# A second pair of up-projection blocks by seven half-size products, and another engine for the opening's ones

## The chip, the cores and the metric

The kernel runs on one core of a Trainium2 chip. The engines are TensorE (PE in the profile; its weight loads are the row PEld), VectorE (DVE), ScalarE (ACT), GpSimd (POOL) and SyncE (SP), which issues most DMAs. Each engine works through its own queue in order and waits on semaphores for the others. The metric is the device time of one execution in microseconds; the median of three runs counts.

## The reference

A two-layer encoder on 512 tokens of width 1024, all in float32. Each layer normalizes, projects, runs three token mixers, gates and merges them, and then applies a convolutional feed-forward block. The change is in the feed-forward block:

```
def conv_ffn(h, w_up, conv_w, conv_b, w_down):
    u = h @ w_up
    C = u.shape[-1]
    u = lax.conv_general_dilated(u, conv_w[:, None, :].astype(u.dtype), window_strides=(1,),
                                 padding=((CONV_W // 2, CONV_W // 2),),
                                 dimension_numbers=('NWC', 'WIO', 'NWC'),
                                 feature_group_count=C) + conv_b
    a, g = jnp.split(u, 2, axis=-1)
    return (jax.nn.gelu(g) * a) @ w_down

def reference(x, ...):
    for l in range(DEPTH):
        h = rmsnorm(x, norm1_g[l])
        x = x + gated_parallel_mixer(h, w_in[l], ...)
        h = rmsnorm(x, norm2_g[l])
        x = x + conv_ffn(h, w_up[l], conv_w[l], conv_b[l], w_down[l])
    return rmsnorm(x, final_g)
```

The up projection is 1024 x 5632: 22 blocks of 128 columns for the half `a` and 22 for the gate half `g`.

## The kernel before

**Products.** Activations stand transposed, 128 channels by 512 tokens. Every float32 operand is split into a high part (fp32r) that ScalarE casts and a low part, the rest, that VectorE subtracts (`split`, lines 208 and 209). A product is three matmuls per 128 channels: high by high, high by low, low by high (`mm3`). For weights the two parts are the tiles `whi` and `wlo`, with three buffers each (`WB`); the raw weights come by SP's queue into `raw`, with three buffers too (`RAWB`). `fetch` issues loads and splits a few weights ahead of their use. The low part of the weights is read by the third matmul of each 128 channels.

**An up block** f of one half (`do_up`) is 8 x 3 matmuls of 512 columns into one PSUM bank, which `conv` reads on ScalarE (line 1113) and twice on VectorE (lines 1115, 1116). A gate block ends in a gelu (line 1120) and a product with its partner (`prod`), and `operands` makes the transformed halves for the down projection (tiles `tt` and `ft`, lines 1141 to 1155).

**A unit** (`do_us`) takes two neighbouring blocks of one half at once. It splits the 2 x 2 block matrix of weights (256 columns by pairs of 128 channels) and the activations (two halves of 256 tokens) as in Strassen's scheme with seven products in place of eight. Each product is 4 x 3 matmuls of 256 columns; the order of the weights is V11, S1, V12, S2, S4, V22, S3. The sums S1 and S3 of raw weights are made by adding DMAs from GpSimd's queue (lines 173, 174), S2 and S4 by VectorE (lines 189, 192). `load_sum` loads V22, V21 (as S1) and V11 into the tiles `own`, `s1`, `own`, and V21 again and V12 into two of the three `raw` buffers; V21's buffer becomes S3 and is held to the last product. The transformed activations are four `hs` tile sets, made once a layer from `hx` (`mix`, `sums4`, lines 1044 to 1048) while blocks 13 and 14 are issued. The tuple `UPS` names the units: before, only blocks 18 and 19 of the gate half.

**Order.** TensorE's and SP's queues follow the program (`schedule`); `ups` alternates the halves. A unit stands where its second block stood. On VectorE and ScalarE a list scheduler places the instructions of blocks 6 and up when the kernel is built; splits of weights have a high priority. In the order before, the blocks of f 16 to 19 are issued as 16a, 16g, 17a, 17g, 18a, 19a, unit 18/19g.

**Banks.** There are eight PSUM banks. In the feed-forward part the group `d` rotates through 0, 1, 2, 3, 4, 5, 7, 6; a dense block takes one, a unit or a sum of the down projection four. Layer 1 opens (`do_mla_open`) with banks 0 to 3 for the first four products, whatever the rotation left. The last sum of layer 0 ends with VectorE's read at line 1185.

**Opening.** Seven idle matmuls (line 432) read a tile of ones, `early`, while the first loads are under way.

Of the kernel before, what the change touches and what calls it, by code (L numbers as in the profile page):

```python
# [24 lines left out]
EPS = 1e-6  # L25
# [14 lines left out]
NP, AHEAD, EVAC = (6, 5, 4), (7, 4), 400  # L40
F2 = 2 * NP[0]
FIX = 6
UPS = ((9, 1),)
ORDERS = (("V11", "S1", "V12", "S2", "S4", "V22", "S3"), ("V11", "V12", "S1", "S2", "S4", "V22", "S3"))
B11, B21, B22, T1, T3, T2, T4 = range(7)
ROWS = (slice(0, 64), slice(64, 128))
# [19 lines left out]
class Trunk:  # L66
# [5 lines left out]
    def __init__(self, ctx, tc, d):  # L72
        self.tc, self.nc, self.d, self.ctx = tc, tc.nc, d, ctx
        nc = self.nc
        self.small = ctx.enter_context(tc.tile_pool(name="small", bufs=1))
        self.const = ctx.enter_context(tc.tile_pool(name="const", bufs=1))
        self.wp = ctx.enter_context(tc.tile_pool(name="wp", bufs=1))
        self.psum = ctx.enter_context(tc.tile_pool(name="psum", bufs=1, space=bass.MemoryType.PSUM))
        self.groups, self.turn = {}, {}
        c = self.const  # L80
        x0 = c.tile([P, S + NPC], F32, name="x0")
        self.x = [x0[:, :S]] + [c.tile([P, S], F32, name=f"x{k}") for k in range(1, KD)]
        self.par = [x0[:, S:], self.small.tile([P, NPC], F32, name="par1")]
        self.early = c.tile([P, P], F32, tag="acc", name="early")
        nc.vector.memset(self.early, 1.0)
        self.idf = c.tile([P, P], F32, name="idf")
        make_identity(nc, self.idf)
        self.mean = c.tile([P, P], F32R, name="mean")
        cst = self.small.tile([P, 7], F32, name="cst")
        self.neghalf, self.ones = cst[:, 0:4], cst[:, 4:5]  # L90
        nc.vector.memset(self.neghalf, -0.5)
        nc.vector.memset(self.ones, 1.0)
        self.eps = cst[:, 6:7]
        nc.vector.memset(self.eps, EPS)
        self.warm = cst[:, 5:6]
        nc.scalar.activation(self.warm, self.ones, AF.Exp)
        self.specs, self.raws, self.parts, self.used = [], {}, [], 0
        self.plans = [self.schedule(l) for l in range(L)]
        for s, W in self.plans:
            self.specs += [w for item in s for w in W.get(item, ())]  # L100
        nc.sync.dma_start(x0[:, :S + PC_CW], d["x0"])
        self.fetch(1, 0)
        for k in range(1, 5):
            nc.sync.dma_start(self.x[k], d["xT"][k * P:(k + 1) * P, :])
            self.fetch(min(k + 1, 3), 0)
        self.gmask = self.small.tile([P, 3 * P], BF16, name="gmask")
# [223 lines left out]
    def schedule(self, l):  # L330
# [30 lines left out]
        for f in ups[8:]:  # L361
            W["up", f] = [(d["w_up"][l], 0, KD, f * P, P)]
        for i, p in UPS:
            unit = {"w": d["w_up"][l], "m": p * NF + 2 * i, "part": 1, "np": 4, "r0": 0, "order": ORDERS[0]}
# [33 lines left out]
        seq[n - 8:n - 8] = [("sum", 0, m) for m in range(0, KD, 2)]  # L398
        for i, p in UPS:
            old = [("up", p * NF + 2 * i + e) for e in range(2)]  # L400
# [97 lines left out]


    def do_mla_open(self):  # L500
        self.banks(g=[0, 1, 2, 3], d=[4, 5, 0, 1, 2, 3], r=[6, 7])
        self.mxs, self.mx = self.open("mx")
        self.mps, self.mp = self.open("ml")
        self.mp2 = self.mps.enter_context(self.tc.tile_pool(name=f"mm{self.l}", bufs=1, reuse_waits="tile"))
        self.rc, self.rsn = (self.mp.tile([P, S], F32, tag=t, name="rope", bufs=2) for t in ("knh", "knl"))
        if self.l:
            self.rope_table()
        self.hb = self.small.tile([P, 24], F32, tag="hb", name="hb")
        self.nc.vector.tensor_scalar(self.hb, self.pr[:, PC_BG:PC_BG + 24], 0.5, None, ALU.mult)
        self.merged, self.z = [None] * KD, {}  # L510
        self.qn, self.kn, self.pts, self.pp, self.y = {}, {}, {}, {}, {}
# [27 lines left out]
    def do_lat4(self):  # L539
        if self.l == 0:  # L540
            rest = self.par[0][:, PC_CW:]
            for t, src in ((rest, self.d["par"][0][:, PC_CW:]), (self.par[1], self.d["par"][1])):
                self.nc.gpsimd.tensor_copy(t[:, 0:4], self.rt)
                self.nc.gpsimd.dma_start(t, src)
            self.nc.gpsimd.tensor_scalar(self.mean, self.idf, 0.0, 1.0 / D, ALU.mult, ALU.add)
        self.latent(4, self.dense(self.spec(), self.h))

# [609 lines left out]
    def do_sum(self, part, m):  # L1157
# [33 lines left out]
        elif m == KD - 2:  # L1191
# [3 lines left out]
            for _ in self.operands(F2):  # L1195
                pass
            if UPS:
                self.whole()
# [219 lines left out]
```

## Time and profile before

| | us |
|---|---|
| median of three runs (1664.78 to 1665.18) | 1665.04 |
| the profiled execution | 1664.89 |
| its span, first to last instruction | 1663.1 |

Over the span the 16 DMA engines move 191 MB at a mean of 115 GB/s. The chain of work that ended last is 97% TensorE. A row of the timeline gives start, duration, engine, line, operation, output<-inputs with shapes, and in brackets the idle time ahead of it with what ended it. A row of the stretches gives the busy time of PE, PEld, DVE, ACT and POOL in it with the number of instructions, then the granted clock, the DMA share and GB/s.

### The profile page before, as it was taken

The numbers are of one execution on the slowest core, as the hardware profiler recorded it, in microseconds if no ns is written. First come the engines' busy times: TensorE is split into PE (matmuls) and PEld (weight loads), VectorE is DVE, ScalarE is ACT, GpSimd is POOL, SyncE is SP. The second block draws the span as 40 slices with busy tenths as digits, with TensorE's granted clock in tenths as the row PEclk, the third lists the DMA queues.
The fourth block names the chain that finished last, engine by engine and source line by source line (L and its number), as shares of the span: only waits on it lengthen the run. The fifth ranks groups of instructions, "written<-read, shape, count | busy, mean of one in ns | idle before, by whom it ended". The sixth has DMA issues, their size and how long they took to land.

```text
span 1663.1 us, 25448 instructions
## 1 busy us (share of the span) xinstructions
PE 1654.7 (99%) x9480; PEld 1415.9 (85%) x9480; DVE 1291.4 (78%) x2256; ACT 948.3 (57%) x1704; POOL 134.1 (8%) x190
## 2 busy tenths in 40 slices
PE   9999999999999999999999999999999999999998
PEld 8888888888898889888987888888889888898888
DVE  7767866787889877797967677667878897777887
ACT  7664545775565544555566545467755655436554
POOL 2122100000000000100011220000001000001000
PEclk9999999999999999999999999999999999999999
DMA  6255523222534366636432564332236343657373
GB/s 183 74 125 114 139 84 95 77 77 74 140 97 133 101 149 155 153 96 165 110 105 80 112 146 106 98 89 77 64 85 150 90 127 101 164 131 175 96 168 94
DMA packets 326923, 191.22 MB, mean 115 GB/s; under 512 B 17072, under 2 KB 313792, under 8 KB 326800
## 3 DMA queue, kind: packets, MB, share of 16 engines
q1 hardware_dynamic: 304064, 162.38, 34.8%
q0 software_dynamic: 22448, 26.89, 9.6%
q8 instruction: 74, 1.21, 0.3%
q14 instruction: 49, 0.40, 0.1%
q10 hardware_dynamic: 288, 0.33, 0.1%
HBM read 168.80 MB, written 2.10 MB: 103 GB/s over the span
## 4 chain that ended last, share of the span: by engine, by line
PE 97%; DVE 1%; ACT 1%; issue 0%; DVEq 0%; ACTq 0%
PE ps_ring L222 13%; PE ps_ring L223 12%; PE ps_ring L224 12%; PE ps_d L222 9%; PE ps_d L224 9%; PE ps_d L223 9%; PE ps_d L1177 5%; PE ps_d L1176 5%; PE ps_d L1175 5%; PE ps_g L222 2%; PE ps_g L224 2%; PE ps_g L223 2%; PE ps_ring L303 2%; PE ps_ring L290 1%; PE ps_ring L792 1%; PE ps_g L323 1%
## 5 line engine op out<-in xcount | busy, mean ns | idle before, releaser
L208 ACT CAST whi<-raw 128x1024 fp32r<-128x1024 f32 (+5 forms) x353 | 291.3, 826 | 351.2 <-PE ps_ring L223 123.4
L209 DVE TENSOR_TENSOR wlo<-raw,whi 128x1024 fp32r<-128x1024 f32 (+5 forms) x351 | 331.4, 946 | 79.4 <-ACT whi L208 77.2
L222 PE MATMUL ps_ring<-hh,whi 128*128 128x512 f32 x600 | 235.6, 393 | 0.6 <-DVE pt L761 0.3
L224 PE MATMUL ps_ring<-hh,wlo 128*128 128x512 f32 x600 | 234.0, 390 | 0.0
L223 PE MATMUL ps_ring<-hl,whi 128*128 128x512 f32 x600 | 233.7, 390 | 0.0
L222 PE MATMUL ps_d<-hh,whi 128*128 128x512 f32 x589 | 229.4, 389 | 0.0
L223 PE MATMUL ps_d<-hl,whi 128*128 128x512 f32 x589 | 229.4, 389 | 0.0
L224 PE MATMUL ps_d<-hh,wlo 128*128 128x512 f32 x589 | 229.3, 389 | 0.0
L1176 PE MATMUL ps_d<-ft,whi 128*128 128x256 f32 x546 | 154.7, 283 | 0.0
L1177 PE MATMUL ps_d<-ft,wlo 128*128 128x256 f32 x546 | 154.7, 283 | 0.0
L1175 PE MATMUL ps_d<-ft,whi 128*128 128x256 f32 x546 | 154.7, 283 | 0.0
L222 PEld LDWEIGHTS ps_ring<-hh,whi 128*128 128x128 f32 x600 | 112.7, 188 | 24.8 <-DVE pt L761 0.6
L224 PEld LDWEIGHTS ps_ring<-hh,wlo 128*128 128x128 f32 x600 | 112.7, 188 | 23.7
L223 PEld LDWEIGHTS ps_ring<-hl,whi 128*128 128x128 f32 x600 | 112.7, 188 | 23.0
L224 PEld LDWEIGHTS ps_d<-hh,wlo 128*128 128x128 f32 x589 | 110.6, 188 | 23.1
L222 PEld LDWEIGHTS ps_d<-hh,whi 128*128 128x128 f32 x589 | 110.6, 188 | 22.7
L223 PEld LDWEIGHTS ps_d<-hl,whi 128*128 128x128 f32 x589 | 110.6, 188 | 22.7
L1176 PEld LDWEIGHTS ps_d<-ft,whi 128*128 128x128 f32 x546 | 104.9, 192 | 0.2
L1175 PEld LDWEIGHTS ps_d<-ft,whi 128*128 128x128 f32 x546 | 104.9, 192 | 0.2
L1177 PEld LDWEIGHTS ps_d<-ft,wlo 128*128 128x128 f32 x546 | 104.9, 192 | 0.0
L215 DVE TENSOR_TENSOR gz<-ps_ring,rb 128x512 f32<-128x512 f32 x44 | 30.4, 691 | 63.2 <-PE ps_ring L224 63.2
L222 PE MATMUL ps_g<-hh,whi 128*128 128x512 f32 x176 | 68.9, 391 | 0.9 <-DVE x L1185 0.9
(419 smaller groups left out, 3578.8 us busy)
## 6 DMA issues: line engine op xcount, KB each, us to landing
raw<-in_w_in_dram SPq DMA_DIRECT2D x86, 512.0 KB, 4.0
raw<-in_w_up_dram SPq DMA_DIRECT2D x68, 512.0 KB, 3.8
raw<-in_w_up_dram SPq DMA_DIRECT2D x36, 256.0 KB, 2.9
raw<-in_w_down_dram SPq DMA_DIRECT2D x18, 384.0 KB, 4.9
tm<-in_namask_dram SPq DMA_DIRECT2D x16, 384.0 KB, 4.3
tm<-in_rpb_dram POOLq DMA_DIRECT2D x48, 128.0 KB, 4.7
own<-in_w_down_dram SPq DMA_DIRECT2D x16, 384.0 KB, 5.9
raw<-in_w_in_dram SPq DMA_DIRECT2D x17, 256.0 KB, 3.2
```

The costliest lines, as they stand in the source:

```text
L208: nc.scalar.copy(hi, src)
L209: nc.vector.tensor_sub(lo, src, r32(hi))
L215: self.nc.vector.tensor_tensor(out, a, b, ALU.mult)
L222: mm(ps, sh, mh, start=first and k == 0, stop=False)
L223: mm(ps, sh, ml, start=False, stop=False)
L224: mm(ps, sl, mh, start=False, stop=last and k == n - 1)
L290: self.nc.tensor.transpose(out[2 * u + i][:, c * 64:c * 64 + 64], block[q], self.idf[q, q])
L303: self.nc.tensor.matmul(out, st[a], mv[b], start=first and t == 0, stop=last and t == 2)
L323: self.nc.tensor.matmul(self.gbank[j], w[:, j * P:(j + 1) * P], m, start=n + t == 0, stop=False)
L1175: mm(ps, wh, hi, start=fresh and i == 0, stop=False, skip_group_check=True)
L1176: mm(ps, wh, lo, start=False, stop=False, skip_group_check=True)
L1177: mm(ps, wl, hi, start=False, stop=i == n - 1, skip_group_check=True)
```

## The change

1. `UPS` gains (8, 1): blocks 16 and 17 of the gate half become a unit too, in both layers. TensorE's order is now 16a, 17a, unit 16/17g, 18a, 19a, unit 18/19g.
2. In layer 1, `do_mla_open` takes its banks in the order in which the rotation would go on.
3. GpSimd writes the tile `early`, and the constant `eps` moves from VectorE's opening to GpSimd.

```
-UPS = ((9, 1),)
+UPS = ((8, 1), (9, 1))
...
-        nc.vector.memset(self.early, 1.0)
+        nc.gpsimd.memset(self.early, 1.0)
...
-        nc.vector.memset(self.eps, EPS)
...
     def do_mla_open(self):
-        self.banks(g=[0, 1, 2, 3], d=[4, 5, 0, 1, 2, 3], r=[6, 7])
+        a = [0, 1, 2, 3, 7, 4, 5, 6]
+        if self.l:
+            a = [self.groups["d"][(self.turn["d"] + i) % 8] for i in range(8)]
+        self.banks(g=a[:4], d=[*a[5:7], *a[:4]], r=[a[7], a[4]])
...
+            self.nc.gpsimd.memset(self.eps, EPS)
             self.nc.gpsimd.tensor_scalar(self.mean, self.idf, 0.0, 1.0 / D, ALU.mult, ALU.add)
```

Line numbers of the changed kernel differ by -1 to +3: its split is lines 207 and 208, the unit's matmuls are 1069 to 1071, the convolution on VectorE is 1118 and 1119.

VectorE, layer 0, before: twelve rows of the stretch in which blocks 16 and 17 are worked off (`wlo` with 1024 columns is the low part of a dense block's weights, `hs` the last transformed activations).

```order
L1047 SCALAR_TENSOR_TENSOR tt<-tt,hx 128x256
L1048 SCALAR_TENSOR_TENSOR tt<-tt,hx 128x256
L209 TENSOR_TENSOR wlo<-raw,whi 128x1024
L215 TENSOR_TENSOR prod<-c 128x512
L1115 SCALAR_TENSOR_TENSOR c<-ps_d,x_67,c 128x511
L209 TENSOR_TENSOR hs<-tt,hs 128x512
L1146 TENSOR_TENSOR tt<-prod 128x512
L1116 SCALAR_TENSOR_TENSOR c<-ps_d,x_67,c 128x511
L1149 TENSOR_TENSOR ft<-prod,ft 128x512
L1150 SCALAR_TENSOR_TENSOR tt<-tt,prod 128x256
L1153 TENSOR_TENSOR ft<-tt,ft 128x512
L1151 SCALAR_TENSOR_TENSOR tt<-tt,prod 128x256
```

The same place now, from the last `hs` to the low part of the unit's fifth product, S4 (`s_7379` is S1 and then S2, the first `raw` is V12 and then S4).

```order
L208 TENSOR_TENSOR hs<-tt,hs 128x512
L1119 SCALAR_TENSOR_TENSOR c<-ps_d,x_67,c 128x511
L1156 TENSOR_TENSOR ft<-tt,ft 128x512
L1153 SCALAR_TENSOR_TENSOR tt<-tt,prod 128x256
L208 TENSOR_TENSOR wlo<-raw,whi 128x512
L1118 SCALAR_TENSOR_TENSOR c<-ps_d,x_67,c 128x511
L1154 SCALAR_TENSOR_TENSOR tt<-tt,prod 128x256
L208 TENSOR_TENSOR wlo<-s_7379,whi 128x512
L191 TENSOR_TENSOR raw<-s_7379,raw 128x512
L1119 SCALAR_TENSOR_TENSOR c<-ps_d,x_67,c 128x511
L1158 TENSOR_TENSOR ft<-tt,ft 128x512
L1078 TENSOR_TENSOR u<-u,ps_d 128x256
```

S4's low part (`L208 wlo<-raw,whi`) is the next row. The unit's splits and sums now stand among the convolutions and transformed halves of the blocks ahead of it. From the last `L1050 tt<-tt,hx` but one (the row that stands at L1047 before) to this row there are 28 instructions: 15 of 512 columns, 6 of 511 and 7 of 256.

VectorE, layer 0, in the unit 18/19, before: from the low part of V12 to that of S2.

```order
L209 TENSOR_TENSOR wlo<-raw,whi 128x512
L1115 SCALAR_TENSOR_TENSOR c<-ps_d,x_67,c 128x511
L192 TENSOR_TENSOR raw<-s_7539,raw 128x512
L209 TENSOR_TENSOR wlo<-s_7539,whi 128x512
L1116 SCALAR_TENSOR_TENSOR c<-ps_d,x_67,c 128x511
```

And now, from V12's to S2's and S4's:

```order
L208 TENSOR_TENSOR wlo<-raw,whi 128x512
L1153 SCALAR_TENSOR_TENSOR tt<-tt,prod 128x256
L1152 TENSOR_TENSOR ft<-prod,ft 128x512
L191 TENSOR_TENSOR raw<-s_7628,raw 128x512
L1154 SCALAR_TENSOR_TENSOR tt<-tt,prod 128x256
L1118 SCALAR_TENSOR_TENSOR c<-ps_d,x_67,c 128x511
L1156 TENSOR_TENSOR ft<-tt,ft 128x512
L208 TENSOR_TENSOR wlo<-s_7628,whi 128x512
L208 TENSOR_TENSOR wlo<-raw,whi 128x512
```

Between V12's and S2's low part there were two rows, now there are six.

SP's queue, layer 0, before: the loads of the up projection behind the first sums.

```order
L140 DMA raw<-in_w_up_dram 128x8x128 x12
L170 DMA own<-in_w_up_dram 128x4x128
L170 DMA s_7539<-in_w_up_dram 128x4x128
L170 DMA own<-in_w_up_dram 128x4x128
L170 DMA raw<-in_w_up_dram 128x4x128 x2
L140 DMA raw<-in_w_up_dram 128x8x128 x4
```

And now (the two dense loads between the units are blocks 18 and 19 of the half a):

```order
L139 DMA raw<-in_w_up_dram 128x8x128 x8
L169 DMA own<-in_w_up_dram 128x4x128
L169 DMA s_7379<-in_w_up_dram 128x4x128
L169 DMA own<-in_w_up_dram 128x4x128
L169 DMA raw<-in_w_up_dram 128x4x128 x2
L139 DMA raw<-in_w_up_dram 128x8x128 x2
L169 DMA own<-in_w_up_dram 128x4x128
L169 DMA s_7628<-in_w_up_dram 128x4x128
L169 DMA own<-in_w_up_dram 128x4x128
L169 DMA raw<-in_w_up_dram 128x4x128 x2
L139 DMA raw<-in_w_up_dram 128x8x128 x4
```

The second unit's five loads moved behind the first unit's and two dense blocks'.

## The prediction

> **What bounds the kernel now.** I read the page's busy shares first, then what PE waited for, then stretches around the places that the change touches.
>
> ```profile
> span 1663.1 us, 25448 instructions
> PE 1654.7 (99%) x9480; PEld 1415.9 (85%) x9480; DVE 1291.4 (78%) x2256; ACT 948.3 (57%) x1704; POOL 134.1 (8%) x190
> PE idle L432 <- DVE cst L92: 1.1, 1, 1.1
> PE ps_g L222 <- DVE x L1185: 0.9, 1, 0.9
> PE ps_ring L222 <- DVE pt L761: 0.6, 4, 0.2
> PE ps_ring L222 <- DVE nm L922: 0.6, 2, 0.3
> PE ps_a L1293 <- ACT o L1305: 0.2, 1, 0.2
> ```
>
> TensorE is busy from end to end; its waits (us in total, times, longest) sum to 3.4 us. So the time moves by what its stream loses in matmuls, plus or minus waits that come or go. None of the five waits lies in the feed-forward part, though VectorE is nearly full just where the new unit goes. By stretch (PE, PEld, DVE, ACT, POOL busy; granted clock), for the four blocks 16 and 17 in layer 0 and in layer 1, and for the unit that exists:
>
> ```profile
> 712.64:734.40 21.76, 21.76 (x98) 18.03 (x96) 21.22 (x34) 12.25 (x19) 1.72 (x2) 1.00 0.61 156
> 1536.57:1558.33 21.76, 21.76 (x97) 18.03 (x96) 21.12 (x33) 12.23 (x18) 1.72 (x2) 1.00 0.60 155
> 745.28:755.35 10.07, 10.07 (x85) 10.07 (x84) 7.83 (x12) 7.38 (x13) 0.00 (x0) 1.00 0.34 99
> ```
>
> VectorE works 21.22 of 21.76 us there: the sums of the transformed activations (lines 1044 to 1048, tiles tt and hs) fall into it. The existing unit stands some 22 us later, where VectorE has gaps.
>
> **TensorE's own work.** Two dense blocks are 48 products of 512 columns; a unit is 84 of 256.
>
> ```profile
> 734.40 0.39 PE L222 MATMUL ps_d<-hh,whi 128*128 128x512 f32 x1
> 745.28 0.28 PE L1066 MATMUL ps_d<-hh,whi 128*128 128x256 f32 x1
> 755.35 0.40 PE L222 MATMUL ps_d<-hh,whi 128*128 128x512 f32 x1
> ```
>
> 48 dense products from 734.40 to 745.28 take 10.88 us (0.227 each), the unit's 84 take 10.07 (0.120 each). Each new unit saves 0.81 us, one in each layer: **-1.62 us**.
>
> **The banks of layer 1's opening.** Each unit draws four PSUM banks where two dense blocks draw two, so the rotation ends layer 0 elsewhere; the change also starts layer 1 on the banks that are next in it. Before, the first bank was the one that the last sum still held:
>
> ```profile
> 828.41 0.28 PE L1177 MATMUL ps_d<-ft,wlo 128*128 128x256 f32 x1
> 828.73 0.69 DVE L1185 TENSOR_TENSOR x<-x,ps_d 128x512 f32<-128x512 f32 x1
> 829.56 0.47 PE L222 MATMUL ps_g<-hh,whi 128*128 128x512 f32 x1 [0.87 <-DVE x L1185]
> ```
>
> The next product could start 0.12 after 828.41, at 828.53, and starts at 829.56: 1.03 us. Counting bank draws in layer 0 (36 up blocks less 4, plus 8 for two units, 16 for the first sums, 2 and 12 behind them) gives 70, so the last sum sits on banks 2 to 5 and layer 1 opens on 7, 6, 0, 1, which are free: **-1.03 us**. What could be late next: nothing near; the opening's first weights and h0 to h3 are made ahead of the last sum's read. Later in layer 1 the attention's fixed ring meets other banks: its first scores then take the bank of the gate read here:
>
> ```profile
> 887.91 0.68 DVE L215 TENSOR_TENSOR gz<-ps_d,rb 128x512 f32<-128x512 f32 x1
> 889.20 0.49 PE L303 MATMUL ps_ring<-kr,qr 64*128 64x512 f32 x1
> ```
>
> That read ends at 888.59, 0.6 us ahead of the scores; it stays covered while VectorE's order there is unchanged, which it is. If that cover goes, some 0.5 us come back; the term's bounds are 0 and -1.1.
>
> **The first new unit waits for low parts.** A product's third matmul needs the low part that VectorE makes of its weights (line 209 before, 208 now). Unit 16, 17 would start at 723.52 (712.64 plus two blocks of 5.44). Its fifth product, S4, starts 4 x 1.44 later and needs its low part 0.24 after that: 729.5. When is it made? VectorE is the same up to 715.15; from there the new order has 28 instructions ahead of S4's low part. How long each holds the queue is read from starts that follow each other with no gap:
>
> ```profile
> 715.15 0.42 DVE L1047 SCALAR_TENSOR_TENSOR tt<-tt,hx 128x256 f32<-128x256 f32 x1
> 715.49 1.22 DVE L209 TENSOR_TENSOR wlo<-raw,whi 128x1024 fp32r<-128x1024 f32 x1
> 716.62 0.43 DVE L1048 SCALAR_TENSOR_TENSOR tt<-tt,hx 128x256 f32<-128x256 f32 x1
> 716.96 0.69 DVE L1044 TENSOR_TENSOR tt<-hx 128x512 f32<-128x512 f32 x1
> 717.56 0.75 DVE L1115 SCALAR_TENSOR_TENSOR c<-ps_d,x,c 128x511 f32<-128x511 f32 x1
> 718.22 0.69 DVE L209 TENSOR_TENSOR hs<-tt,hs 128x512 fp32r<-128x512 f32 x1
> ```
>
> 256 columns 0.34, 1024 columns 1.13, 512 columns 0.60, 511 columns 0.66. The 28 are 15 of 512, 6 of 511 and 7 of 256: 9.00 + 3.96 + 2.38 = 15.34 us. So S4's low part runs from 730.49 to 731.18, against a need at 729.5: TensorE loses about **1.7 us** (0.4 of it already at the products before). Their inputs are in time: ScalarE's cast of V12 can start when block 17 frees its buffer (723.5), that of S4 when VectorE has summed it (729.0); at 0.62 each (a row further down) they are done 1 us or so ahead of VectorE's. In layer 1 the queue stands 0.19 better, since this VectorE row comes at 1538.89 (823.74 later) and the old unit at 1569.21 (823.93 later): **1.5 us**. Bounds: 1.3 and 2.0 each.
>
> ```profile
> 1538.89 0.43 DVE L1047 SCALAR_TENSOR_TENSOR tt<-tt,hx 128x256 f32<-128x256 f32 x1
> 1569.21 0.28 PE L1066 MATMUL ps_d<-hh,whi 128*128 128x256 f32 x1
> ```
>
> **The old unit waits too.** Only two dense blocks now lie between the units. Raw weights have three buffers, and a unit holds one until its last product's low part is split (V21's buffer, which becomes S3). The load of block 19's weights waits for it, and on SP's queue the five loads of unit 18, 19 stand behind that load; two adding DMAs on POOL's queue follow. S3's low part is the second row behind S4's: done at 731.18 + 0.60 + 0.60, about 732.4. A load that was waited for took this long:
>
> ```profile
> 752.49 0.37 SPq L140 DMA_DIRECT2D raw<-in_w_up_dram  x1
> 756.38 1.05 ACT L208 CAST whi<-raw 128x1024 fp32r<-128x1024 f32 x1 [0.85 <-DMA raw<-in_w_up_dram]
> 717.78 0.50 SPq L170 DMA_DIRECT2D s<-in_w_up_dram  x1
> 723.02 0.86 POOL L173 DMA_DIRECT2D s<-own  x1 [33.24 <-DVE prod L215]
> s<-own POOLq DMA_DIRECT2D x1, 256.0 KB, 3.3
> ```
>
> 3.89 us to the cast and 1.05 for it: block 19's low part can start at 737.4, in time for TensorE (740.8). But VectorE then has that row (1.13), 8 of 0.60 and 5 of 0.66 ahead of V12's low part, 9.2 us, with about 1.0 of waits for ScalarE in them (a gelu and two casts): V12's starts at 747.7. (S1 is added in time: its load is issued at 733.4, the adding DMA follows 5.24 later and lands in 3.3, the cast takes 0.62: 742.6; its row comes at 743.3.) From there six rows stand ahead of S2's low part where two stood before: 0.60 + 0.34 + 0.60 + 0.60 + 0.34 + 0.66 + 0.60 = 3.74, so it is done at 752.1. The unit starts at 746.2 (the first wait included) and needs it 3 x 1.44 + 0.24 later, at 750.8: **1.35 us** in each layer. Even with VectorE not behind it would be 0.5, from how the old unit's V12 was split at once when its buffer came free:
>
> ```profile
> 745.25 0.62 ACT L208 CAST whi<-raw 128x512 fp32r<-128x512 f32 x1 [3.10 <-PE ps_d L223]
> 745.91 0.69 DVE L209 TENSOR_TENSOR wlo<-raw,whi 128x512 fp32r<-128x512 f32 x1 [1.29 <-ACT whi L208]
> ```
>
> 0.63 after the unit's start, plus 3.74 and 0.69, is 5.06 against 4.56. Bounds: 0.5 and 1.9 (the load 0.6 later).
>
> **The opening.**
>
> ```profile
> 0.73 0.20 POOL masks.py:197 MEMSET idf<- 128x128 f32 x1 [0.29 <-POOLq L1406]
> 0.83 0.17 DVE L85 MEMSET early<- 128x128 f32 x1 [0.83 <-PEq L1406]
> 1.05 3.36 PE L432 MATMUL idle<-early 128*128 128x128 f32 x14 [1.05 <-DVE cst L92]
> 4.41 2.70 PEld L323 LDWEIGHTS ps_g<-h,whi 128*128 128x128 f32 x8 [0.29 <-ACT h L467]
> 4.44 3.11 PE L323 MATMUL ps_g<-h,whi 128*128 128x512 f32 x8
> 7.39 1.07 PE L323 MATMUL ps_g<-h,wlo 128*128 128x512 f32 x4
> 21.90 0.60 PE L251 MATMUL ps_r<-idf,acc 128*128 128x128 f32 x4
> ```
>
> GpSimd would fill its first tile from 0.73 to 0.93, 0.07 ahead of VectorE's 1.00. The idle matmuls start as much earlier, but the first product waits for h (0.29 idle), which hangs on the load of x: I take 0. GpSimd's identity comes 0.2 later and is first read at 21.9; eps moves to an idle engine. The eight products from 4.44 to 7.39 stand 0.37 apart, the later ones (0.227, above) closer: TensorE starts slow. If it came up to speed ahead of them, 8 x (0.37 - 0.227) = 1.1 us would go; if later, as much could come. Bounds: -1.1 and +1.1.
>
> The Trainium skill, "TensorE: Matmul & The Clock Gate", section "What's actually happening", says that the array runs at half rate until one window of about 3.4 us, which starts at no fixed time, has been busy. The spacing here agrees with a slow start, though the granted clock reads full throughout. By it a start 0.07 us earlier moves the change of speed to an earlier window in about 0.07 of 3.4 cases: an estimate of 2%.
>
> **The sum.** -1.62 - 1.03 + 1.7 + 1.5 + 2 x 1.35 + 0 = **+3.25 us**. The profiled execution took 1664.89 (its span and 1.79 around it), 0.15 under the median of the runs shown: 1668.14, or 1668.3 from the median; I say 1668.2. With the waits at their bounds, 1.3 + 1.3 + 1.0 and 2.0 + 2.0 + 3.8, it is +0.95 to +5.15.
>
> **Rivals.**
> - **TensorE never waits** (faster): the low parts come in time, and only -2.65 stands: 1662.2. It needs S4's low part 1.7 us earlier. For it: TensorE has not one wait in the feed-forward part now, with VectorE as full. Against: there, 22 us of VectorE work had 22 us; the new unit puts seven splits and two sums into it with a need every 1.44 us. It decides at three rows fewer ahead of S4, or rows a tenth shorter.
> - **One of the two waits alone**: the queue recovers between the units (a load of 3 us in place of 3.9, or ScalarE's waits overlap), or the first wait is smaller: 1.5 to 2.7 us less, 1665.5 to 1666.7.
> - **The loads of unit 18, 19 come later still**: they stand behind block 19's on SP's queue, and each us that S1's adding DMA is late behind 743.3 pushes VectorE's rows and both units' ends by as much. At 1 us or more in both layers: 1670.2 and above.
> - **The opening changes speed in another window**: 1.1 us either way on any of these; 0.03, spread over them.
>
> **How the numbers follow.** The sum of the walk 0.60 (1666.7 to 1669.5), never waits 0.18, one wait alone 0.14, later loads 0.08. The range goes from never waits to the upper bound less the rare end: 1662.1 to 1669.8. About 0.2% of the time (3.3 us) is what a measurement can tell from no change: slower from 1668.4, faster below 1661.7. The walk's case lies astride the first, 0.27 above and 0.33 below; never waits gives 0.02 faster and 0.16 the same; with the others: faster 0.03, same 0.62, slower 0.35.
>
> **What would show it.** The waits of TensorE in the changed profile should name line 208's wlo at lines 1069 to 1071, 1.7 us near 730 and 1.5 some 825 us later, most of it at S4, and 1.35 some 21 us behind each, at S2. Layer 1's first product should follow the last sum's by 0.12. Block 19's cast should wait for its load. The prediction is wrong if the units stand at 10.07 us each, if VectorE's order has gaps before S4, or if waits stand elsewhere, the ring of layer 1 above all.

## The result and the profile after

| | us |
|---|---|
| before, median of 4 executions (1664.78 to 1665.18) | 1665.10 |
| after, median of 4 executions (1671.74 to 1674.42) | 1673.74 |
| after, the profiled execution | 1674.42 |
| its span, first to last instruction | 1672.6 |

After against before is 1.005, with a 95% interval of 1.0033 to 1.0068: 8.6 us slower. The prediction had 1668.2 and a range up to 1669.8. The four executions of after lie 2.7 us apart, those of before 0.4.

The page of after, its first two lines:

```profile
span 1672.6 us, 25674 instructions
PE 1657.5 (99%) x9552; PEld 1418.9 (85%) x9552; DVE 1298.6 (78%) x2274; ACT 955.6 (57%) x1722; POOL 137.8 (8%) x196
```

Busy shares do not tell the two kernels apart. What TensorE waited for does (us in total, times, longest):

```profile
PE ps_d L1071 <- DVE wlo L208: 6.3, 6, 1.9
PE idle L431 <- POOL early L85: 1.0, 1, 1.0
PE ps_ring L221 <- DVE pt L764: 0.6, 4, 0.2
PE ps_ring L221 <- DVE nm L925: 0.6, 2, 0.3
PE ps_ring L223 <- DVE wlo L208: 0.5, 1, 0.5
```

The wait on x at layer 1's opening is gone, and the units' third matmuls (line 1071) wait six times for low parts. How long each unit takes is read from stretches of after that begin with its first matmul and end with the next block's; the third row is a part of the second unit of layer 0 (PE, PEld, DVE, ACT, POOL busy; granted clock, DMA share, GB/s):

```profile
724.46:736.48 12.02, 10.86 (x85) 10.28 (x84) 11.13 (x19) 7.11 (x13) 0.00 (x0) 1.00 0.26 75
747.39:761.63 14.24, 12.18 (x85) 11.72 (x84) 12.98 (x23) 9.26 (x17) 0.00 (x0) 0.88 0.26 75
755.80:759.20 3.40, 3.40 (x18) 3.40 (x17) 2.49 (x5) 1.67 (x3) 0.00 (x0) 0.50 0.56 163
1552.81:1564.98 12.17, 10.84 (x85) 10.27 (x84) 11.29 (x20) 6.88 (x12) 0.00 (x0) 1.00 0.27 73
1575.89:1588.65 12.76, 10.69 (x85) 10.22 (x84) 12.51 (x22) 8.53 (x16) 0.00 (x0) 1.00 0.23 66
```

And where layer 1 opens in after, the last matmul of the sums, the first product, and VectorE's read of the sum:

```profile
834.69 0.28 PE L1180 MATMUL ps_d<-ft,wlo 128*128 128x256 f32 x1
834.81 0.40 PE L221 MATMUL ps_g<-hh,whi 128*128 128x512 f32 x1
835.01 0.69 DVE L1188 TENSOR_TENSOR x<-x,ps_d 128x512 f32<-128x512 f32 x1
```

The product follows by 0.12, ahead of the read. A unit without waits takes 10.07 us. Whatever a unit takes beyond that it loses: the first units (layer 0, layer 1) 1.95 and 2.10, the second ones 4.17 and 2.69. Of the 4.17, 1.5 are no wait: for 3.4 us the granted clock is 0.50, and 16 matmuls follow each other at 0.213 us in place of 0.12.

The sum for the profiled executions, in us:

| term | predicted | measured |
|---|---|---|
| TensorE's own work | -1.62 | -1.62 |
| layer 1's opening | -1.03 | -1.03 |
| first units' waits | 1.7 + 1.5 | 1.95 + 2.10 |
| second units' waits | 1.35 + 1.35 | 2.7 + 2.69 |
| half clock in layer 0's second unit | not in the sum | 1.5 |
| layer 0 up to 437 us (same matmul in both traces) | 0 | 0.94 |
| the rest, in small steps | 0 | 0.3 |
| sum | 3.25 | 9.5 |

The 0.94 is mostly one wait for the low part of a weight at 155.39 (the row on line 223 above; the matmul starts 0.75 late) whose load landed later. Two other profiled executions with the same code there, experiments 1 and 2 below, do not have it.

### The profile page after: what moved, and what is told of

It reads as the page before. It is cut to its first block, busy times and chain, and to the rows that moved or that the text cites. A ratio compares the mean times of both kernels' runs of the same rounds, so it can differ in the third digit from the quotient of the medians.

```text
span 1672.6 us, 25674 instructions
## 1 busy us (share of the span) xinstructions
PE 1657.5 (99%) x9552; PEld 1418.9 (85%) x9552; DVE 1298.6 (78%) x2274; ACT 955.6 (57%) x1722; POOL 137.8 (8%) x196
## 4 chain that ended last, share of the span: by engine, by line
PE 90%; DVE 5%; DMA 2%; issue 1%; ACT 1%; SPq 0%; DVEq 0%; POOL 0%; ACTq 0%; POOLq 0%
PE ps_ring L221 12%; PE ps_ring L222 12%; PE ps_ring L223 12%; PE ps_d L222 8%; PE ps_d L221 8%; PE ps_d L223 8%; PE ps_d L1179 5%; PE ps_d L1178 5%; PE ps_d L1180 5%; PE ps_g L223 2%; PE ps_g L221 2%; PE ps_g L222 2%; PE ps_ring L302 2%; PE ps_ring L289 1%; DVE wlo L208 1%
## 5 line engine op out<-in xcount | busy, mean ns | idle before, releaser
L207 ACT CAST whi<-raw 128x1024 fp32r<-128x1024 f32 (+4 forms) x355 | 291.5, 821 | 351.1 <-PE ps_ring L222 125.2
L208 DVE TENSOR_TENSOR wlo<-raw,whi 128x1024 fp32r<-128x1024 f32 (+4 forms) x353 | 330.6, 938 | 76.9 <-ACT whi L207 75.0
L221 PE MATMUL ps_d<-hh,whi 128*128 128x512 f32 x557 | 216.8, 389 | 0.0
L222 PE MATMUL ps_d<-hl,whi 128*128 128x512 f32 x557 | 216.8, 389 | 0.0
L223 PE MATMUL ps_d<-hh,wlo 128*128 128x512 f32 x557 | 216.7, 389 | 0.0
L223 PEld LDWEIGHTS ps_d<-hh,wlo 128*128 128x128 f32 x557 | 104.6, 188 | 21.8
L221 PEld LDWEIGHTS ps_d<-hh,whi 128*128 128x128 f32 x557 | 104.6, 188 | 21.7
L222 PEld LDWEIGHTS ps_d<-hl,whi 128*128 128x128 f32 x557 | 104.6, 188 | 21.3
L223 PE MATMUL ps_g<-hh,wlo 128*128 128x512 f32 x176 | 68.8, 391 | 0.0
```

The lines of the kernel that those rows point to most:

```text
L207: nc.scalar.copy(hi, src)
L208: nc.vector.tensor_sub(lo, src, r32(hi))
L221: mm(ps, sh, mh, start=first and k == 0, stop=False)
L222: mm(ps, sh, ml, start=False, stop=False)
L223: mm(ps, sl, mh, start=False, stop=last and k == n - 1)
```

## Where the second unit's wait comes from

The walk of the prediction gave times for each row of VectorE's queue. After's queues, in order: SP, GpSimd, VectorE, TensorE.

```profile
732.69 0.58 SPq L169 DMA_DIRECT2D own<-in_w_up_dram  x1
733.32 0.50 SPq L169 DMA_DIRECT2D s<-in_w_up_dram  x1
738.56 0.86 POOL L172 DMA_DIRECT2D s<-own  x1 [30.54 <-DMA s<-in_w_up_dram]
737.32 1.23 DVE L208 TENSOR_TENSOR wlo<-raw,whi 128x1024 fp32r<-128x1024 f32 x1 [0.67 <-ACT whi L207]
745.54 0.69 DVE L208 TENSOR_TENSOR wlo<-s,whi 128x512 fp32r<-128x512 f32 x1 [2.11 <-ACT whi L207]
750.05 0.68 DVE L208 TENSOR_TENSOR wlo<-raw,whi 128x512 fp32r<-128x512 f32 x1
753.78 0.69 DVE L208 TENSOR_TENSOR wlo<-s,whi 128x512 fp32r<-128x512 f32 x1
754.53 0.39 PE L1071 MATMUL ps_d<-hs,wlo 128*128 128x256 f32 x1 [1.93 <-DVE wlo L208]
```

Up to 738.6 the walk holds to 0.1 us: S1's load at 733.32 (predicted 733.4), its adding DMA 5.24 later, block 19's low part at 737.32 (737.4). That is partly luck, as these three rows of after show (S4's low part, block 19's load, S3's low part):

```profile
731.56 0.69 DVE L208 TENSOR_TENSOR wlo<-raw,whi 128x512 fp32r<-128x512 f32 x1
732.27 0.37 SPq L139 DMA_DIRECT2D raw<-in_w_up_dram  x1
732.76 0.69 DVE L208 TENSOR_TENSOR wlo<-raw,whi 128x512 fp32r<-128x512 f32 x1
```

The prediction had block 19's load wait for S3's low part. It starts ahead of that row, as soon as S4's low part is done (732.25). S4's low part was 1.1 us later than predicted, and the two errors cancel.

Then S1's low part comes at 745.54 in place of 743.3, and VectorE has stood idle 2.11 us in front of it. From there all rows are late by that, V12's (747.7 predicted) and S2's. The unit itself also starts 1.2 later than the walk had it (747.39 in place of 746.2, mostly the 0.94 above), which by luck gives half of the lateness back: without the 2.11 the same rows would end at 752.36, 0.4 behind a need at 751.95. Transfers of after issued between 730 and 750 us (KB each, median us from issue to landing):

```profile
raw<-in_w_up_dram SPq DMA_DIRECT2D x2, 512.0 KB, 4.5
own<-in_w_up_dram SPq DMA_DIRECT2D x2, 256.0 KB, 4.7
raw<-in_w_up_dram SPq DMA_DIRECT2D x2, 256.0 KB, 5.4
s<-in_w_up_dram SPq DMA_DIRECT2D x1, 256.0 KB, 4.6
s<-own POOLq DMA_DIRECT2D x1, 256.0 KB, 6.3
```

The adding DMA took 6.3 us where the prediction, from the kernel before, had 3.3. Seven loads, block 19's and those that stood behind it on SP's queue among them, are issued within 6.5 us (to 738.58). Three of them are still under way when the adding DMA is issued at 738.56, the seventh goes out with it, and S3's adding DMA joins at 740.34. In the 6.3 us 1.37 MB move, at a DMA share of 0.98; in the 3.3 us of the kernel before it was 0.52 MB at 0.74.

In layer 1 the lateness has two parts. VectorE's rows for block 19's and S1's low parts:

```profile
1566.68 1.23 DVE L208 TENSOR_TENSOR wlo<-raw,whi 128x1024 fp32r<-128x1024 f32 x1 [1.53 <-ACT whi L207]
1574.06 0.69 DVE L208 TENSOR_TENSOR wlo<-s,whi 128x512 fp32r<-128x512 f32 x1 [1.27 <-ACT whi L207]
```

Block 19's load takes 4.7 us there in place of 3.9, so VectorE already stands idle for 1.53 in front of that row (0.67 in layer 0). S1's adding DMA takes 5.4, and 1.27 more are lost in front of S1.

## What put VectorE behind

The first unit's wait had a longer history. A row of VectorE in after, the first one that reads the tiles hx:

```profile
691.84 0.69 DVE L1047 TENSOR_TENSOR tt<-hx 128x512 f32<-128x512 f32 x1 [7.94 <-DMA hx<-hl]
```

VectorE stands idle for 7.94 us until this row can start, since eight adding DMAs make its input, and then works on with about 1 us of idle time to the unit 32 us later. In the kernel before the same row has 7.80 of idle time, at 690.75, and costs nothing, since its only unit stands later. This row gave a way to move VectorE's whole queue without touching the unit, and the experiments use it.

## The experiments

Theory: the units wait because VectorE is behind (from the wait for hx) and because S1's adding DMA shares the DMA engines with the loads released just before it; the half clock follows from the wait. Rivals: VectorE's order next to the units makes the waits by itself; the moved fills or the banks cost something; the half clock has another cause. The kernels ran in three groups, each beside executions of the kernel before.

| run | this, us | before, us | ratio, 95% interval |
|---|---|---|---|
| 1 one unit as before, banks and fills | 1665.04 | 1665.07 | 1.0001 (0.9992 to 1.001) |
| 2 only unit 16/17 | 1668.42 | 1665.07 | 1.002 (1.0012 to 1.0029) |
| 3 earlier loads for unit 18/19 | 1667.37 | 1665.07 | 1.0017 (1.0008 to 1.0025) |
| 4 filler in the wait | 1670.53 | 1665.07 | 1.0032 (1.002 to 1.0044) |
| 5 after again | 1673.02 | 1665.04 | 1.0046 (1.0032 to 1.006) |
| 6 hx by VectorE | 1669.52 | 1665.04 | 1.0027 (1.0017 to 1.0038) |
| 7 hx by VectorE and earlier loads | 1664.40 | 1665.04 | 0.9995 (0.9986 to 1.0004) |
| 8 before, hx by VectorE | 1665.06 | 1665.04 | 1.0001 (0.9992 to 1.001) |
| 9 as 7, V22 third | 1665.19 | 1665.27 | 1.0 (0.9991 to 1.0008) |
| 10 as 9, old banks | 1664.69 | 1665.27 | 0.9996 (0.9987 to 1.0005) |
| 11 hx by VectorE and filler | 1667.48 | 1665.27 | 1.0013 (1.0005 to 1.0022) |
| 12 before, fills moved | 1665.79 | 1665.27 | 1.0002 (0.9994 to 1.0011) |

**1. Banks and fills without the new unit.**

```
-UPS = ((8, 1), (9, 1))
+UPS = ((9, 1),)
```

> The changed kernel with one unit again (blocks 18 and 19), so only the bank order of layer 1's opening and the moved fills of early and eps remain. Walk: before less 1.03 us for the bank wait, opening 0: about 1664.1, TensorE's wait on x at layer 1's opening gone, the unit 10.07 us long. Rival 1 (the moved fills cost something in the opening or later in layer 0): 1664.6 to 1665.2, with a wait in layer 0 that the kernel before does not have. Rival 2 (the bank wait comes back in the rings of layer 1): 1665.1, with a new wait on ps_ring.

1665.04, and the second rival's wait is there: layer 1's opening has none, and one comes in the rings. The profile of this run:

```profile
883.89 0.39 PE L223 MATMUL ps_d<-hh,wlo 128*128 128x512 f32 x1
884.38 0.69 DVE L214 TENSOR_TENSOR ev<-ps_d,rbk 128x512 f32<-128x512 f32 x1 [3.91 <-POOL rbk L267]
885.21 0.47 PE L221 MATMUL ps_ring<-mg,whi 128*128 128x512 f32 x1 [0.93 <-DVE ev L214]
```

With one unit the rotation ends on other banks, and a ring product meets the bank from which VectorE still reads; the start comes 1.32 after the last one, where it is 0.23 without a wait. The gain of 1.03 is given back. With two units (after) this wait is not there.

**2. The first unit alone.**

```
-UPS = ((8, 1), (9, 1))
+UPS = ((8, 1),)
```

> The changed kernel with the unit 16/17 alone; 18 and 19 are dense. One unit a layer, so TensorE's own work is that of the kernel before. Theory (the first unit is late by its own place in VectorE's queue, whatever follows it): waits of 1.95 and 2.1 us remain, less 1.03 for the bank: 1665.1 + 4.05 - 1.03 = 1668.1; no half-clock stretch, as no single wait is over 1.3 us. Rival (the second unit's rows and loads make the first late too): waits under 0.5 each, 1664.1 to 1665.

1668.42, as the theory has it, though partly for another reason. The units lose 2.09 and 1.90, so the first unit's wait does not need the second. The ring's wait of run 1 is here too (1.58 between starts), where the expectation had the bank's gain whole. In the profiled execution an earlier opening, 0.7 ahead of before at 435.67, makes up for half of it; for the median it is not shown what does.

**3. The loads of V22, V21 for S1, and V11 ahead of block 19's load.** `load_parts` issues these three loads and S1's adding DMA; only the order of these transfers on SP's and GpSimd's queues differs from after.

```
+            if ahead and spec[0] != "sum" and ahead[0][0] == "sum" and ahead[0][2].get("early"):
+                self.load_parts(ahead[0][2])
             self.raws[len(self.raws)] = ...
```

> The changed kernel; only SP's order differs: the loads of V22, V21 for S1, and V11 of the unit 18/19 stand ahead of block 19's load, which waits for a raw buffer. Theory (the adding DMA for S1 took 6.3 us because seven loads shared the DMA engines with it, and VectorE then stood 2.1 us in front of S1's low part): the adding DMA lands in about 3.3 us and ahead of need, VectorE's wait of 2.1 us is gone, the unit 18/19 waits 0.2 to 0.5 us for S2's low part in place of 2.65, and no half-clock stretch follows: 1673.7 - 2 x 2.3 - 1.2 = about 1668. Rival (the six rows ahead of S2's low part in VectorE's order make the wait, whatever the load does): 1672.5 to 1674, the wait at S2 still over 2 us.

1667.37 against 1668. The transfer in the same stretch of this run:

```profile
s<-own POOLq DMA_DIRECT2D x1, 256.0 KB, 3.2
```

It takes 3.2 us in place of 6.3, and the second units lose 0.65 and 1.46 in place of 2.7 and 2.69. VectorE's order is that of after, row by row, so order alone does not make this wait: with it unchanged, 0.65 of 2.7 are left in layer 0 and 1.46 of 2.69 in layer 1. The run moves loads and adding DMA together and does not part the two adding DMAs' share in the traffic from that of the loads. The expected 0.2 to 0.5 was too low; in layer 1 block 19's load again takes 4.9, and VectorE stands idle for 1.67 in front of its low part. The first unit lost 0.81 and 2.36 in this profile, and its hx landed early in layer 0 (6.81 us of idle time in place of 7.94).

**4. Sixteen unread matmuls in the wait.**

```
+            if (f2, j) == (9, 3):
+                free = self.groups["d"][self.turn["d"] % 8]
+                idle = self.psum.tile([P, S], F32, tag=f"b{free}", name="idle")
+                for _ in range(16):
+                    mm(idle[:, :256], self.h[0][0][:, :P], self.h[0][0][:, :256], start=True, stop=True)
```

> The changed kernel with 16 matmuls of 256 columns, read by nobody, ahead of product S2 of the unit 18/19 in each layer, about 1.9 us of TensorE work in the 2.2 us in which it waits there anyway. Theory (the stretch of 3.4 us at half clock follows from the wait, when the wait falls into one window of the clock): the waits cost the same, the clock stays full in every run: 1671.5 to 1672.2, with a spread under 0.6. Rival 1 (the half clock has another cause): 1673.7 as before, with clocks of 0.998 and 0.999 in most runs. Rival 2 (the filler is not hidden): 2 x 1.9 more, 1675 and above.

1670.53, under the range. The granted clock is 1.000 in five of six executions and 0.999 in one. The profile of this run shows that layer 0's first unit lost only 0.90, again with an earlier hx, so the filler's share of the 3 us is not clean here; run 11 repeats it where the first wait is gone.

**5. After once more.**

> The changed kernel once more, unaltered, for its spread beside the runs below. Theory (the half clock of 3.4 us comes with some executions only, and the first unit's wait hangs on when an adding DMA lands): between 1670 and 1675, with steps of about 1.5 between executions. Rival (the time is as fixed as that of the kernel before): 1673.7 with a spread under 0.8.

Five executions: 1671.15, 1671.58, 1673.02, 1673.91, 1675.07, with granted clocks of 0.999, and 0.998 in the slowest. The spread of 3.9 is as the theory has it, the clean steps are not seen. The half clock is one thing that moves it (this run's profile has it too, in layer 0's second unit); the landing of hx is probably another, which no run here measures by itself.

**6. hx by VectorE.**

```
-            self.nc.scalar.copy(part, r32(self.h[k][0]))
-            self.nc.gpsimd.dma_start(part, r32(self.h[k][1]), accum_op=ALU.add)
+            self.nc.vector.tensor_add(part, r32(self.h[k][0]), r32(self.h[k][1]))
```

> The changed kernel; only the tiles hx are made in another way: VectorE adds hh and hl itself, eight adds of 512 columns, 4.8 us, in place of ScalarE's copies and GpSimd's adding DMAs. Theory (VectorE stands idle for 7.9 us from 683.9 to 691.8 behind the first row that reads hx, and is behind TensorE from there to the units): it comes out of the adds about 3 us earlier, the first unit's waits of 1.95 and 2.1 go, block 19's load is issued up to 2 us earlier and the unit 18/19 waits 0.5 to 1 in place of 2.65, and no half-clock stretch follows: 1673.7 - 4.05 - 3.8 - 1.2 = about 1664.6. Rival (the rows next to S4's and S2's low parts make the waits, whenever the queue starts): 1673 or more, as VectorE has 9.6 us more to do.

VectorE in this run, layer 0:

```profile
682.06 4.90 DVE L1028 TENSOR_TENSOR hx<-hh,hl 128x512 f32<-128x512 f32 x8
686.87 1.22 DVE L208 TENSOR_TENSOR wlo<-raw,whi 128x1024 fp32r<-128x1024 f32 x1
688.01 0.68 DVE L1143 TENSOR_TENSOR ft<-prod,ft 128x512 fp32r<-128x512 f32 x1
688.61 0.68 DVE L1046 TENSOR_TENSOR tt<-hx 128x512 f32<-128x512 f32 x1
...
743.72 0.69 DVE L208 TENSOR_TENSOR wlo<-s,whi 128x512 fp32r<-128x512 f32 x1 [2.10 <-ACT whi L207]
```

The first row on hx starts 3.2 us earlier, and both first units take 10.07: their waits are gone, 4.05 us in all, with 9.6 us more of VectorE work. The second half of the expectation fell: the second units still lose 2.48 and 2.72, so 1669.52 and not 1664.6. The loads behind block 19's are issued 1.7 us earlier, but the unit starts 1.6 earlier too (745.78), the adding DMA still takes 6.2 and VectorE still stands 2.10 in front of S1.

**7. Both.**

> The last kernel together with the earlier loads of V22, S1 and V11 of the unit 18/19. Theory: no wait of either unit is left; what remains is TensorE's own gain and the bank: 1665.1 - 1.62 - 1.03 = 1662.4, and the spread is that of the kernel before. Rival (as many rows stand ahead of S2's low part, so 0.5 to 1 us is left in each layer whatever is landed): 1663.5 to 1664.5.

1664.40, in the rival's range, 8.6 under after in the same group and 0.6 under before, which is inside the interval of no difference. The first units lose nothing, the second 0.65 and 1.25. ScalarE, VectorE and TensorE in this run, where the second unit begins at 744.21:

```profile
744.18 0.62 ACT L223 CAST whi<-raw 128x512 fp32r<-128x512 f32 x1 [2.21 <-PE ps_d L238]
744.83 0.69 DVE L224 TENSOR_TENSOR wlo<-raw,whi 128x512 fp32r<-128x512 f32 x1 [0.34 <-ACT whi L223]
748.58 0.68 DVE L224 TENSOR_TENSOR wlo<-s,whi 128x512 fp32r<-128x512 f32 x1
```

Now V12's cast waits for its weight buffer, VectorE waits for the cast, and S2's low part is done 5.05 after the unit's start, against a need at 4.56. That is the 0.5 that the prediction gave for the case of a VectorE that is not behind. In layer 1 VectorE is behind by 0.6 even so: it starts V12's low part 1.24 after the unit's start, without idle time ahead of it, where layer 0 has 0.62. Block 19's load took 4.7 us there, as in after.

**8. Control.** The kernel before with the edit of run 6.

> Control: the kernel before with hx by VectorE in the same way. Theory (its one unit has slack, so VectorE's idle time there costs it nothing): 1665.0, within 0.5 of before. Rival (hx by VectorE is a gain or a loss by itself, as by 16 adding DMAs less or 9.6 us more of VectorE): 1663 or 1667.

1665.06: with slack ahead of its one unit, VectorE's idle time costs nothing, and hx by VectorE is no gain by itself.

**9. V22 as third product.** Run 7 with the order changed.

```
+UNIT = ("V11", "S1", "V22", "V12", "S2", "S4", "S3")
-        steps = ((B11, 0), (T1, 1), (B21, 2), (T2, 0), (B22, 1), (T4, 3), (T3, 0))
+        steps = ((B11, 0), (T1, 1), (T4, 3), (B21, 2), (T2, 0), (B22, 1), (T3, 0))
```

> The kernel with hx by VectorE and the early loads (1664.40), with V22 as third product of both units in place of sixth, so that VectorE's order has two rows between the low parts of V12 and S2 where it had six, and V22's low part hangs on no sum. Theory (what is left, 0.65 and 1.26 us at S2, is the rows between V12's and S2's low parts): it goes, 1664.4 - 1.9 = 1662.5. Rival (the weight buffers free too late for any order): 1664 to 1664.5, with the wait at another product.

No gain, 1665.19 beside 1665.27. The units lose 0.15, 0.86, 0.16 and 0.70, 1.87 in all where run 7 lost 1.90; the waits stand at V12 and S4 now. The order moved the wait and did not take it away. Whether the three weight buffers are the floor was not tried and stays open.

**10. The banks of layer 1's opening as before.** Run 9 with the old line in `do_mla_open`.

> The last kernel with the banks of layer 1's opening as in the kernel before. Theory (the bank order takes a wait of 1.03 us away and nothing gives it back with two units): 1.0 slower than the last kernel, with TensorE's wait on x at layer 1's first product. Rival (the wait comes back elsewhere in layer 1 anyway): within 0.3 of the last kernel.

1664.69, not 1.0 slower, and TensorE's list has no wait on x. TensorE and VectorE where layer 1 opens:

```profile
830.06 0.28 PE L1193 MATMUL ps_d<-ft,wlo 128*128 128x256 f32 x1
830.18 0.40 PE L238 MATMUL ps_g<-hh,whi 128*128 128x512 f32 x1
830.38 0.69 DVE L1201 TENSOR_TENSOR x<-x,ps_d 128x512 f32<-128x512 f32 x1
```

The next product follows by 0.12 with the old banks. The second unit alone moves the last sum off the banks that layer 1 opens on; the edit of the bank order adds nothing to it. The term of -1.03 came as predicted, and the second unit suffices as its cause.

**11. The filler where the first wait is gone.** Run 6 with the matmuls of run 4.

> The changed kernel with hx by VectorE (1669.52, with granted clocks of 0.997 and 0.998 in five of seven executions and 1.000 in the two fastest, 1668.55 and 1668.87), and 16 matmuls of 256 columns, read by nobody, ahead of product S2 of the unit 18/19 in each layer, in its wait of 2.2 us. Theory (the half clock follows from the wait): clocks of 0.999 or 1.000 in every execution and 1668.3 to 1669.0, with a spread under 1. Rival 1 (another cause): 1669.5 with clocks of 0.997 and 0.998. Rival 2 (the filler adds its time): 1672 or more.

Clocks of 0.999 or 1.000 in all eleven executions, where run 6 had 0.997 or 0.998 in five of seven. A mean of 0.999 alone could hide one half-clock stretch (3.4 us at 0.50 lowers the mean by 0.001), but 14 of the 33 executions of before beside it have 0.999 too, the profiled execution (0.999) has the full clock from 6.16 to 1665.04 us, and the other executions with 0.999 (1667.12 to 1667.66) are no slower than those with 1.000 (1666.63 to 1667.74). 2.2 over its before where run 6 was 4.5 over: the filler, 1.92 us of matmuls in each layer, makes the kernel 2 us faster. It came out 0.8 under the range, which I took from run 6's two executions at full clock; the profiled one of these stood 1.3 behind before at 437 us, which may explain it.

**12. The fills alone.**

```
-        nc.vector.memset(self.early, 1.0)
+        nc.gpsimd.memset(self.early, 1.0)
...
-        nc.vector.memset(self.eps, EPS)
...
+            self.nc.gpsimd.memset(self.eps, EPS)
```

> The kernel before with only the fills moved: early by GpSimd, eps by GpSimd. Theory (the first product waits for h, which hangs on the load of x): no change, 1665.0, within 0.4. Rival (the earlier idle matmuls bring TensorE up to speed a window sooner): 1664.0.

1665.79, 0.5 over its before, inside the interval of no difference. In run 1 they came with 1665.04. No gain is seen; the interval's upper end, 1.0011, leaves room for a loss of 1.8.

## Why the prediction failed, step by step

- **TensorE's own work**: right; the unit takes 10.07 wherever it does not wait (run 6).
- **Layer 1's opening**: right in size; the cause is the unit's banks (run 10), and the edit of the bank order is not needed. Alone it gives the gain back in the rings (run 1), which the prediction looked for at another row.
- **The first unit waits**: right in place and mechanism, the largest wait at S4. 1.95 and 2.10 stand against 1.7 and 1.5, within the bounds of 1.3 and 2.0 in one layer and 0.1 outside in the other. Ahead of the queue that was counted stands the wait for hx (run 6); it varies by about 1 us between profiles (6.81 to 8.11 us of idle time in layer 0 of after and runs 1 to 5), and this term with it.
- **The old unit waits too**: the step that failed. The walk put S1's adding DMA at 3.3 us, a row taken where the DMA share was 0.74. Beside four loads and a second adding DMA (share 0.98) it took 6.3, VectorE stood 2.11 in front of S1, and the wait is 2.7 in place of 1.35. In layer 1 the adding DMA took 5.4 and block 19's load 4.7 in place of 3.9, with 2.69 in place of 1.35. Run 3 brings the DMA back to 3.2 and the waits to 0.65 and 1.46. The buffer that block 19's load waits for was wrong too (S4's, not S3's), which luck made good. One rival had this chain and its price (each us that S1 is late moves both ends) with 1670.2 and above, but looked for the lateness in when the loads are issued, not in how long the transfer takes when they come together, and had a chance of 0.08.
- **The half clock**: a second step that failed, a term that was not in the sum at all, though the prediction had the granted clock in its rows. 1.5 us in the profiled execution. The opening had been searched for this, the waits that the prediction itself forecast had not.
- **The opening**: 0 is consistent with runs 1 and 12; profiled executions of changed kernels stand between 0.7 ahead of and 1.5 behind before at 437 us, so a single profile says nothing on it.

## What to carry to other kernels

A transfer's duration belongs to the traffic beside it (here 3.2 to 6.3 us for the same 256 KB): where a change holds loads back and then releases them together, take the price from a stretch with that traffic, or bound it by the bytes that land in it. When an engine's queue is behind, follow it back to the wait that put it behind; here it stood 32 us ahead of the place that paid. And a wait of TensorE can cost twice: here one of 2.2 us halved the clock behind it in some executions, so a forecast that has such a wait needs that term or a chance for it.

## What the hardware showed

The granted clock goes by windows. In the record of after it rises at 4.87, falls at 755.81, rises at 759.22 and falls at 1670.58: full for 750.93 and 911.36 us, 220 and 267 times the 3.413 us that the half clock lasted. On this grid, after's stretches around the long waits of layer 0 and layer 1:

```profile
748.98:752.39 3.41, 3.28 (x27) 3.02 (x25) 3.38 (x7) 2.92 (x7) 0.00 (x0) 1.00 0.00 0
752.39:755.81 3.42, 1.49 (x12) 1.29 (x12) 3.42 (x7) 1.64 (x3) 0.00 (x0) 1.00 0.00 0
755.81:759.22 3.41, 3.41 (x18) 3.41 (x17) 2.48 (x5) 1.69 (x3) 0.00 (x0) 0.50 0.57 164
...
1578.42:1581.83 3.41, 2.55 (x19) 2.08 (x17) 3.41 (x8) 3.38 (x8) 0.00 (x0) 1.00 0.00 0
1581.83:1585.24 3.41, 2.20 (x18) 2.20 (x19) 3.41 (x7) 1.54 (x4) 0.00 (x0) 1.00 0.11 30
```

In layer 0 the wait of 2.2 us falls into one window, TensorE is busy for 1.49 of 3.42, and the next window has half the clock. In layer 1 a wait as long lies across two windows, busy for 2.55 and 2.20, and nothing follows. Two other profiles have waits as long. The window of layer 0 on the grid of run 5, then those of layer 0 and layer 1 on the grid of run 6:

```profile
752.53:755.95 3.42, 1.55 (x13) 1.55 (x14) 3.42 (x7) 1.54 (x4) 0.00 (x0) 1.00 0.00 0
...
750.94:754.36 3.42, 1.65 (x13) 1.65 (x14) 3.42 (x7) 1.54 (x4) 0.00 (x0) 1.00 0.01 2
1573.56:1576.97 3.41, 1.86 (x13) 1.54 (x12) 3.41 (x8) 3.38 (x8) 0.00 (x0) 1.00 0.00 0
```

The half clock follows the first (1.55 busy) and neither of the others (1.65 and 1.86). This agrees with a limit on the busy time within one window, between 1.55 and 1.65 of 3.42 us by these few profiles, and not with a limit on the length of a wait. Where the grid lies differs between executions (the first rise stands between 4.5 and 6.8 us in the profiles here), so the same wait costs 1.5 us more in some executions and not in others: this is part of after's spread. The Trainium skill, "TensorE: Matmul & The Clock Gate", section "What's actually happening", has a free-running window of 3413 ns, and the trace agrees. Its section "Why this matters for your kernels" advises against idle gaps over about 3 us; here 2.2 us were enough.
